# One streaming encoder layer on one core: a third natural tile, weight sums held back in issue order, other visit sizes for the adaptive product, another opening order

## The chip, the cores and the metric

The kernel runs on one core of one Trainium2 chip. Its engines work side by side, each through its own queue in order: TensorE (PE, with weight loads PEld), VectorE (DVE), ScalarE (ACT), GpSimd (POOL) and SyncE (SP), which here only issues transfers (DMAs). The metric is device time in microseconds (us), lower is better.

## The reference

One layer of an encoder is computed for two request groups: a prompt of 1024 rows and a sample of 32 rows with 512 cached rows. Width is 1024, everything is float32.

```python
ada = silu(c) @ w_ada + b_ada              # six vectors of 1024 for each group
h = rms_norm(x, g_pre_mix) * (1 + sc1) + sh1
p = h @ w_in                               # 1024 x 4256: latents, rope key, SB q, k, v, two gates
o_a = latent attention (softmax)           # 8 heads, chunk mask
o_b = stick-breaking attention             # 8 heads of 64, causal
merged = sigmoid(g_a) * (o_a @ w_proj_a) + sigmoid(g_b) * (o_b @ w_proj_b)
x = x + gt1 * rms_norm(merged @ w_out, g_post_mix)
x = x + gt2 * rms_norm(conv_ffn(rms_norm(x, g_pre_ffn) * (1 + sc2) + sh2), g_post_ffn)
```

Besides the two outputs, the new key and value rows of both branches and the last rows of the convolution are returned. The change touches the computation of `ada`, the first normalisation `h`, the part of `h @ w_in` that gives q, k and v of the stick-breaking branch, and the loads with which that branch's attention begins.

## The kernel before

Each float32 operand of the large products is split into a rounded half ("hi", ScalarE, line 96) and a remainder ("lo", VectorE, line 99), and a product is three matmuls. Most of the program is written in Tile, a language in which a planner sets the issue order of each engine from the program order and its own costs; where it says `manual_schedule`, PE, ACT and DVE keep the order of the program. Each tag of a pool has so many buffers; a tile waits until the last reader of the buffer's former tile is done, and a pool laid over the space of a released one waits tile by tile.

*Opening (`stage_h`, manual order).* Eight tiles of 128 rows of x come in. For each, `scale` takes the sum of squares on ScalarE (L136), the power on POOL (L128, L129) and the multiplication on VectorE (L414). `ada_half` is the product that gives shift and scale for one half of the columns, in eight steps whose weights are loaded as they are used (L293, L296), and then transposes (L302). `norm_T` takes four tiles of rows and half of the columns: for each of four column blocks it transposes on TensorE (`turn_x`, L315), and `put` (L324) writes scale and shift, once in full and once rounded, on ScalarE; the remainder is VectorE's. `each(n, m, ...)` runs one step of each in that order. `Plain` are the first products with plain weights (L550, read out at L73).

*The strips (`stage_in`, planned).* The product for q, k and v is made by a scheme that saves one product in eight: for each pair of 128-column strips there are seven half-size products, `step_a` to `step_g`, each of 24 matmuls (L550). Its sums of weight halves are taken on VectorE: `sum_1` (L569) adds two halves, `sums_w` (L589, L590) and `sum_4` (L594) overwrite them. `z_out` (L558, L560) reads results out of PSUM, with copies on ScalarE or sums on VectorE; steps d, e and f accumulate in one pair of banks, which is read between them. There are six such groups (n = 2 to 7, called strips 2 to 7 below). Weights of even ones lie in `wr`, of odd ones in `S`, two buffers each. `z_done` stores a finished strip. For k and v it transposes back to rows (L741), copies to a "natural" tile `nat` (L743, two buffers) and stores that (L748); for v it also splits into `hs` (L752, L753, two buffers) and stores that to `vd` (L754).

*Stick-breaking attention (`stage_sb`, PE, ACT and DVE in the written list `ORDER`).* `sb_load` (L789) loads for each of a pair's two heads the keys (KH, twice), the keys' remainder (KLz), the queries (Q, twice), and V for both. Its pool `sb` lies over those of T1, T3 and T2, the operands of steps b, e and d. In `ORDER`, f is one step of filling work from `gates`: products of the gate columns (L103 to L105). Each of the 12 gate strips has 32 of these steps and, ahead of its third block, one visit of `ada_step`: 3, 3 and 2 steps in turn, each with one load of 128 rows of `w_ada` and four matmuls (L245, loads L229, L234 for the bias). The first tile of a visit is `wa`, the others are `wr`, which the gate weights (L113) also use. The sum is added at D (L250).

## Time and profile before

| | |
|---|---|
| median of three runs | 1762.36 us (1761.33 to 1766.96) |
| the profiled execution's own time | 1761.96 us |
| its span, first to last instruction | 1759.9 us |
| granted TensorE clock over the span | 0.987 |
| PE busy / DVE busy / ACT busy / POOL busy | 1691.3 / 1260.4 / 928.5 / 300.3 us |
| stages named below (us from the start of the span) | opening and first products to about 97, strips to 251, stick-breaking attention from 251 |

A row of the waits names who waited, for whom, and us in total, times, longest. A row in order of time begins with the start and the length in us; brackets hold the idle time ahead of it on its engine and what ended it. Rows of SPq are issues of transfers. Several equal neighbours are merged (x2). A busy TensorE is not one at full clock: the granted clock stands in a column of its own.

### The profile page before, as it was taken

How to read it: one execution, taken by the hardware profiler on the slowest of the kernel's cores; microseconds unless marked ns; L12 is line 12 of the kernel's file. 1: busy time of each engine (PE TensorE's matmuls, PEld its weight loads, DVE VectorE, ACT ScalarE, POOL GpSimd, SP SyncE). 2: the span in 40 equal slices, each digit the busy share in tenths (PEclk: the TensorE clock that was granted, in tenths of full speed). 3: DMA queues.
4: the chain of work that ended last, by engine and by line, in shares of the span. 5: the costliest groups of instructions: out<-in, count | busy, mean ns of one | idle time of the engine just before them, and what ended most of it. 6: DMA issues, size and time to landing. Idle time of an engine off the chain costs nothing. (4 is left out here: it accounts for less than half of the span.)

```text
span 1759.9 us, 31441 instructions
## 1 busy us (share of the span) xinstructions
PE 1691.3 (96%) x12184; PEld 1540.8 (88%) x12184; DVE 1260.4 (72%) x2083; ACT 928.5 (53%) x1804; POOL 300.3 (17%) x622
## 2 busy tenths in 40 slices
PE   5899898999999999999999999999999999999997
PEld 2898897998999989889888879999999999977886
DVE  3585556887784477776777668977877787788556
ACT  5533334565564567767676267544444454444442
POOL 2103231211111001111100032211111111210013
PEclk8999999999999999999999999999999999999999
DMA  9335388564543222121237532343334323597753
GB/s 329 129 94 182 114 262 251 175 182 143 159 120 88 73 62 72 47 87 63 67 121 256 157 133 78 116 138 126 115 101 138 126 91 126 189 344 250 236 147 117
DMA packets 177928, 255.32 MB, mean 145 GB/s; under 512 B 14043, under 2 KB 118484, under 8 KB 176756
## 3 DMA queue, kind: packets, MB, share of 16 engines
q1 hardware_dynamic: 158900, 194.90, 35.5%
q0 software_dynamic: 18656, 58.34, 9.2%
q8 instruction: 96, 1.57, 0.4%
q14 instruction: 52, 0.43, 0.1%
q10 hardware_dynamic: 224, 0.09, 0.0%
HBM read 186.76 MB, written 65.99 MB: 144 GB/s over the span
## 5 line engine op out<-in xcount | busy, mean ns | idle before, releaser
L96 ACT ACTIVATE wh<-wr 128x1024 fp32r<-128x1024 f32 (+6 forms) x164 | 132.2, 816 | 239.0 <-PE s L2028 78.5
L99 DVE TENSOR_TENSOR wl<-wr,wh 128x1024 fp32r<-128x1024 f32 (+5 forms) x161 | 151.1, 945 | 94.7 <-ACT wh L96 93.5
L103 PE MATMUL mm<-H,wh 128*128 128x264 f32 x348 | 102.6, 295 | 0.0
L105 PE MATMUL mm<-H,wl 128*128 128x264 f32 x348 | 99.9, 287 | 0.0
L104 PE MATMUL mm<-H,wh 128*128 128x264 f32 x348 | 99.6, 286 | 0.0
L2029 PE MATMUL s<-T,wl 128*128 128x256 f32 (+1 forms) x328 | 93.7, 286 | 0.0
L2027 PE MATMUL s<-T,wh 128*128 128x256 f32 (+1 forms) x328 | 93.3, 284 | 0.0
L2028 PE MATMUL s<-T,wh 128*128 128x256 f32 (+1 forms) x328 | 93.2, 284 | 0.0
L99 DVE TENSOR_TENSOR PTl<-tr,PTh 128x512 fp32r<-128x512 f32 x100 | 68.2, 685 | 29.6 <-ACT PTh L96 29.0
L2168 DVE SCALAR_TENSOR_TENSOR u<-u,c,u 128x1058 f32<-128x1058 f32 x68 | 87.0, 1316 | 1.9 <-ACT u L2165 0.7
L99 DVE TENSOR_TENSOR wl<-S,wh 128x1024 fp32r<-128x1024 f32 (+1 forms) x58 | 60.9, 1056 | 35.5 <-ACT wh L96 35.4
L925 PE MATMUL tr<-c,A 128*128 128x128 f32 x576 | 83.8, 275 | 1.1 <-DVE A L1027 0.5
L2027 PE MATMUL tr<-T,wh 128*128 128x272 f32 (+1 forms) x272 | 77.8, 286 | 0.0
L2029 PE MATMUL tr<-T,wl 128*128 128x272 f32 (+1 forms) x272 | 77.7, 286 | 0.0
L96 ACT ACTIVATE wh<-S 128x1024 fp32r<-128x1024 f32 (+1 forms) x58 | 53.4, 926 | 45.7 <-PE s L2028 13.4
L2028 PE MATMUL tr<-T,wh 128*128 128x272 f32 (+1 forms) x272 | 77.5, 285 | 0.0
L96 ACT ACTIVATE PTh<-tr 128x512 fp32r<-128x512 f32 x100 | 59.3, 598 | 32.0 <-PE tr L925 28.6
L886 DVE TENSOR_TENSOR_SCAN M<-M,tab 128x512 f32<-128x512 f32 (+4 forms) x64 | 58.6, 916 | 21.2 <-ACT M L871 21.0
L925 PEld LDWEIGHTS tr<-c,A 128*128 128x128 f32 x576 | 65.6, 141 | 9.2 <-issue 2.1
L2029 PE MATMUL mm<-T,wl 128*128 128x256 f32 (+1 forms) x256 | 73.0, 286 | 0.3 <-DVE wl L99 0.2
L2027 PE MATMUL mm<-T,wh 128*128 128x256 f32 (+1 forms) x256 | 73.1, 286 | 0.0
L2028 PE MATMUL mm<-T,wh 128*128 128x272 f32 (+1 forms) x256 | 72.8, 285 | 0.0
(820 smaller groups left out, 6222.3 us busy)
## 6 DMA issues: line engine op xcount, KB each, us to landing
wr<-in_w_up_dram SPq DMA_DIRECT2D x44, 512.0 KB
dr<-in_w_down_dram SPq DMA_DIRECT2D x43, 512.0 KB
wr<-in_w_ada_dram SPq DMA_DIRECT2D x33, 512.0 KB
wr<-gdn SPq DMA_DIRECT2D x30, 512.0 KB
wr<-in_w_in_dram SPq DMA_DIRECT2D x27, 512.0 KB
gdn<-u POOLq DMA_DIRECT2D x23, 512.0 KB, 4.8
t<-gd SPq DMA_DIRECT2D x16, 528.0 KB
d<-in_w_down_dram SPq DMA_DIRECT2D x16, 512.0 KB
```

Source lines behind the costliest of these rows:

```text
L96: self.nc.scalar.activation(out, in_, AF.Identity, scale=scale)
L99: return self.nc.vector.tensor_tensor(out, full, hi.bitcast(F32), ALU.subtract)
L103: m(ps, lh, rh, start=start, stop=False)
L104: m(ps, lh, rl, start=False, stop=False)
L105: self.pe = m(ps, ll, rh, start=False, stop=stop).ins
L886: self.nc.vector.tensor_tensor_scan(r, r, tab[:, ::-1], 0.0, ALU.mult, ALU.max)
L925: self.nc.tensor.transpose(tr[:, (2 * s + q) * P : (2 * s + q + 1) * P], at[q][:, b * P : b * P + P], self.idt)
L2027: m(ps[:, :n], w[0][:, k], x[0][:, k, c], start=first and k == 0, stop=False, skip_group_check=True)
L2028: m(ps[:, :n], w[0][:, k], x[1][:, k, c], start=False, stop=False, skip_group_check=True)
L2029: i = m(ps[:, :n], w[1][:, k], x[0][:, k, c], start=False, stop=k == 3, skip_group_check=True)
L2168: nc.vector.scalar_tensor_tensor(y, u[:, w : w + YW], self.cvT[:, w, cc : cc + 1], y, ALU.mult, ALU.add)
```

## The change

- `nat` gets three buffers, `q1` two in place of three.
- `sum_1` is put behind the last output of the group before (`f_out`, the second L560 of `step_f`) in VectorE's issue order. For the first group there is none.
- The visits of `ada_step` for the first pair of heads do 1, 3 and 4 steps in 3, 3 and 2 turns of the fill; for the later pairs as before 3, 3 and 2. Where there are fewer steps than turns, a turn is empty; where more, the last steps fall into one turn. The fourth tile of a visit lies in an `A` buffer of the attention.
- The load for the first visit is issued after the loads of both heads in place of after V; `wa` is allocated ahead of Q and KH in the pool `sb`.
- Opening: for the first half of the columns the rounded put of every odd block goes to VectorE (`put_v`). The `scale` of tiles 4 to 7 comes between the four steps of the first `norm_T`, ahead of the first product, in place of after it. Steps of the second `norm_T` (n) and of `ada_half` (m) run n n m m n m m n m m m m in place of n m m n m m n m m n m m.

```diff
@@ ada_load
-        w = self.tl(pool, [P, D], F32, "wr") if i else self.tl(self.Sp, [P, D], F32, "wa", 1)
+        w = self.tl(*((self.Sp, [P, D], F32, "wa", 1), (pool, [P, D], F32, "wr"), (pool, [P, D], F32, "wr"),
+                      (self.At, [P, TP], F32, "A"))[i])
@@ ada_step
+        n, turns = n
...
-            if i < n - 1:
+            if i < min(n, turns) - 1:
                 yield
+        for _ in range(turns - n):
+            yield
@@ norm_T
+        def put_v(out, x, q):
+            nc.vector.tensor_scalar(out, x, g[:, q, 0:1], self.adaT[:, 0, q, 0:1], ALU.mult, ALU.add)
...
-                put(H[0][:, k, c], x, q)
+                (put if hf or k % 2 == 0 else put_v)(H[0][:, k, c], x, q)
@@ stage_h
                 n = norm(0, 0, turned)
-                each(n, n, n, n)
+                for t in range(4, 8):
+                    each(n)
+                    scale(t)
                 A.go(0, 0, "mm", 0)
-                for t in range(4, 8):
-                    scale(t)
                 n = norm(4, 0)
-                each(n, m, m, n, m, m)
-                each(n, m, m, n, m, m)
+                each(n, n, m, m, n, m, m, n, m, m, m, m)
@@ z_out
-                self.nc.scalar.copy(out[:, c], ps[:, :n])
+                r = self.nc.scalar.copy(out[:, c], ps[:, :n])
             else:
-                self.nc.vector.tensor_tensor(out[:, c], ps[:, :n], x[:, c], ALU.add)
+                r = self.nc.vector.tensor_tensor(out[:, c], ps[:, :n], x[:, c], ALU.add)
+        return r
@@ step_a
-        g["q1"] = self.z_q("q1", 3)
+        g["q1"] = self.z_q("q1", 2)
@@ sum_1
-        self.nc.vector.tensor_tensor(s, g["rb"][:, :512], g["rb"][:, 512:], ALU.add)
+        with self.tc.issue_after(self.f_out.ins) if self.f_out else ExitStack():
+            self.nc.vector.tensor_tensor(s, g["rb"][:, :512], g["rb"][:, 512:], ALU.add)
@@ step_f
-        self.z_out(g["ub"][:, :HC], g["X"], g["q1"])
+        self.f_out = self.z_out(g["ub"][:, :HC], g["X"], g["q1"])
@@ z_done
-            st = self.tl(self.Zp, [P, n * P], F32, "nat" if n > 1 else "nat1", 2 if n > 1 else 1)
+            st = self.tl(self.Zp, [P, n * P], F32, "nat" if n > 1 else "nat1", 3 if n > 1 else 1)
@@ sb_load
-                if p == 0:
-                    self.ada_w = [self.ada_load(self.W, self.At, 0, *self.ada_todo[0])]
+        if p == 0:
+            self.ada_w = [self.ada_load(self.W, self.At, 0, *self.ada_todo[0])]
@@ gates
-                        yield from self.ada_step((3, 3, 2)[i % 3], self.W, self.At, ada)
+                        yield from self.ada_step(((1, 3), (3, 3), (4, 2))[i] if i < 3 else ((3, 3), (3, 3), (2, 2))[i % 3], self.W, self.At, ada)
@@ stage_sb
-        for n, shape, dt in (("M", [P, TP + 8], F32), ("V", [P, 8, 2, P], F32R), ("Q", [P, TP], F32R), ("KH", [P, TP], F32R)):
-            self.tl(S, shape, dt, n, {"V": 1, "KH": 2, "Q": 3}.get(n))
+        for n, shape, dt in (("M", [P, TP + 8], F32), ("V", [P, 8, 2, P], F32R), ("wa", [P, D], F32), ("Q", [P, TP], F32R),
+                             ("KH", [P, TP], F32R)):
+            self.tl(S, shape, dt, n, {"V": 1, "KH": 2, "Q": 3, "wa": 1}.get(n))
```

More of the change, by code (lines that the diff above doesn't have):

```diff
@@ L335, in norm_T @@
                 put(f, x, q)
-                put(H[0][:, k, c], x, q)
+                (put if hf or k % 2 == 0 else put_v)(H[0][:, k, c], x, q)
                 self.lo(H[1][:, k, c], f, H[0][:, k, c])
                 if t0:
-                    nc.vector.tensor_scalar(edge[:, k], tr[:, 0:16], g[:, q, 0:1], self.adaT[:, 0, q, 0:1], ALU.mult, ALU.add)
+                    put_v(edge[:, k], tr[:, 0:16], q)
                     if k % 2:
@@ L400, in stage_h @@
         self.B = ((B11, B12), (B21, B22))
-        self.n_unit, self.S, self.done = 0, [], []
+        self.n_unit, self.S, self.done, self.f_out = 0, [], [], None
         self.Z = dict(B11=B11, B21=B21, B22=B22)
```

## The prediction

> **What bounds the kernel now.** I read the page's first part, then TensorE's (PE's) waits grouped by line, then the busy times of chosen stretches with their granted clock, and last the instructions in order of time around each long wait. The page first:

> ```profile
> span 1759.9 us, 31441 instructions
> ...
> PE 1691.3 (96%) x12184; PEld 1540.8 (88%) x12184; DVE 1260.4 (72%) x2083; ACT 928.5 (53%) x1804; POOL 300.3 (17%) x622
> ```

> TensorE is busy for 1691.3 of 1759.9 us, and the change takes no matmul away. All it can win is 68.6 us of idle time and what a slower clock costs after it. TensorE's waits, the longest groups that the changed lines touch:

> ```profile
> PE mm L245 <- DMA wr<-in_w_ada_dram: 6.0, 2, 5.6
> PE tr L741 <- ACT nat L743: 5.6, 3, 3.7
> PE tr L315 <- DVE x L414: 4.2, 4, 1.3
> PE mm L550 <- DVE u L560: 3.9, 1, 3.9
> ...
> PE s L816 <- DMA Q<-qld: 2.2, 1, 2.2
> ```

> They are five places: the adaptive matmuls (L245), the natural tiles (L741), the opening (L315), the strip sums (L550) and the first attention loads (L816). Each costs more than its wait, because the granted clock falls behind it. These are stretches (start:end, length, busy us per engine with counts, then granted clock, DMA share, GB/s):

> ```profile
> 22.00:37.00 15.00, 7.51 (x26) 4.11 (x28) 7.67 (x13) 11.00 (x18) 4.32 (x8) 0.64 1.05 381
> 145.40:149.40 4.00, 4.00 (x21) 4.00 (x22) 1.68 (x4) 0.58 (x1) 1.75 (x2) 0.57 0.80 282
> 198.80:204.00 5.20, 5.19 (x24) 5.19 (x25) 2.53 (x5) 0.00 (x0) 0.00 (x0) 0.53 0.00 0
> 253.70:259.00 5.30, 5.29 (x30) 5.30 (x31) 2.70 (x7) 1.56 (x6) 0.00 (x0) 0.68 1.12 400
> 273.30:279.00 5.70, 5.27 (x32) 3.58 (x32) 0.42 (x1) 0.00 (x0) 0.00 (x0) 0.52 0.72 210
> ```

> TensorE is full in the last four, at 0.57, 0.53, 0.68 and 0.52 of its clock. Lost work is the length times what is missing: 4.0 x 0.43 = 1.7, 5.2 x 0.47 = 2.4, 5.3 x 0.32 = 1.7 and 5.7 x 0.48 = 2.7 us. With the waits in front of them the places are worth: A (natural tile) 3.7 + 1.7 = 5.4; B (sum) 3.9 + 2.4 = 6.3; C (first load) 2.2 + 1.7 = 3.9; D (adaptive) 6.0 + 2.7 = 8.7 us. Two more waits of L741 make up 5.6 - 3.7 = 1.9 us.

> [...]

> **The change, part by part.** The sum is made against the profiled execution's own 1761.96 us, 0.4 us under the median of the three runs, 1762.36.

> *Third natural tile (place A).*

> ```profile
> 145.36 0.28 PE L741 MATMUL tr<-c,u 128*32 128x128 f32 x1 [3.74 <-ACT nat L743]
> ...
> 149.94 0.28 PE L550 MATMUL mm<-b12h,wh 128*128 128x256 f32 x1
> ...
> 144.72 1.26 ACT L743 COPY nat<-tr 128x512 f32<-128x512 f32 x2 [5.95 <-DMA out_dram<-nat]
> ...
> 146.63 0.43 DVE L752 CAST hs<-nat 128x512 fp32r<-128x512 f32 x1 [1.50 <-DMA vd<-hs]
> 148.15 0.42 DVE L560 TENSOR_TENSOR u<-mm,q 128x256 f32<-128x256 f32 x1 [1.09 <-DMA out_dram<-nat]
> ...
> 140.36 1.15 POOL L754 DMA_DIRECT2D vd<-hs  x2 [0.36 <-DVE hs L753]
> ```

> At 145.36 TensorE has waited 3.74 us: the third copy out of PSUM (144.72) waits until the store of the first natural tile lands. With three tiles that copy need not wait, and TensorE goes on at 141.6. What is late next is on VectorE: its cast of the third tile (146.63) waits for the store of V, issued at 140.36 from the two `hs` tiles, which nobody adds to; and the sum of step e (148.15) is queued behind that cast. Step e takes 149.94 - 145.36 = 4.6 us, less 1.7 of slow clock 2.9, so it would end at 144.5; its first output would come at 146.63 + 0.43 + 0.42 = 147.5, and step f waits 3.0 us for it. Then A wins 5.4 - 3.0 = 2.4, and 0.7 if the clock falls again for 1.7. If the planner puts the sum ahead of the cast, it wins all 5.4. Nothing in the trace decides the order; I take 3.0. The two small waits: bounds 0 and 1.9, I take 1.0, the middle. The tile's space comes from the third `q1`. The next strip's `q1` is written after step f, the last reader of the older one, so two are enough: 0.

> *Held sums (place B).*

> ```profile
> 196.99 0.69 DVE L569 TENSOR_TENSOR s<-S 128x512 f32<-128x512 f32 x1 [4.53 <-DMA S<-in_w_in_dram]
> ...
> 198.33 0.43 DVE L560 TENSOR_TENSOR u<-mm,q 128x272 f32<-128x272 f32 x1
> ...
> 201.70 0.63 PE L550 MATMUL s<-H,wh 128*128 128x256 f32 x2
> ...
> 208.45 0.29 PE L550 MATMUL s<-t1h,wh 128*128 128x256 f32 x1
> ...
> 205.59 1.16 ACT L96 ACTIVATE wh<-wr 128x512 fp32r<-128x512 f32 x2 [11.01 <-PE pv L550]
> ```

> The sum of strip 7's weight halves (L569) sits on VectorE's queue in the middle of strip 5 and waits 4.53 us for its weights; step e's second output (198.33) is queued behind it, and step f waits 3.9 us for that. Held until strip 6's step f has given its output, the sum is far behind its weights' landing. L589, which overwrites what it reads, is held with it. Cover: from the end of step f (201.70) to step b (208.45) TensorE has 6.75 us of steps g and a. In it must fit the output 0.43, the sum 0.69, ScalarE's rounding 1.16 / 2 = 0.58 and VectorE's remainder, of the sum's size, 0.69: 2.4 us. If the cover is gone, step b waits. Bounds 4.0 (2.3 us of other work of VectorE then lies in front of step e) and 6.3; I take 6.0.

> *Attention's opening (C, and the first visit of D).*

> ```profile
> SPq L789 <- PE mm L550: 21.1, 3, 20.0
> ...
> 242.29 1.15 SPq L789 DMA_DIRECT2D KH<-khd  x2
> ...
> 244.64 1.02 SPq L789 DMA_DIRECT2D Q<-qhd  x1
> ...
> 246.98 0.42 SPq L229 DMA_DIRECT2D wa<-in_w_ada_dram  x1
> ...
> 263.43 0.45 SPq L789 DMA_DIRECT2D Q<-qhd  x1
> 264.96 0.45 SPq L789 DMA_DIRECT2D Q<-qld  x1
> 266.37 0.94 SPq L229 DMA_DIRECT2D wr<-in_w_ada_dram  x2
> ...
> 263.46 0.64 PE L245 MATMUL mm<-wa,cT 128*32 128x256 f32 x8 [0.32 <-DMA wa<-in_w_ada_dram]
> ...
> 300.09 0.64 PE L245 MATMUL mm<-wr,cT 128*32 128x256 f32 x8
> ...
> 320.75 0.64 PE L245 MATMUL mm<-wa,cT 128*32 128x256 f32 x8
> ```

> SyncE's first load (KH, 242.29) waits 20.0 us for TensorE. The pool's tiles lie over T1, T3 and T2 in the order of their first allocation. By the sizes in the code, the first KH (4,096 bytes a partition) covers the end of T2, which step d of the last strip reads until that moment; its last 512 bytes are T1's. With `wa` put ahead of Q and KH, everything behind moves by 4,096 bytes: both KH and both KLz come to lie on T1, free since step b, and only Q and `wa` wait for T2. So KH (2 x 256 KB) leaves before 242.29, and Q behind it meets a shorter queue. Q left at 244.64; up to 2.35 us of that can go, plus the time of 512 KB. The wait of 2.2 us is covered by either; its clock may not be. Bounds 0 (SyncE keeps its old order) and 3.9; I take 3.0.

> Place D: the first visit now does one step, from the tile loaded ahead, and two empty turns. The two `wr` loads issued only at 266.37 are no longer needed there: 6.0 + 2.7 us. Their 16 matmuls are done at the third visit, which adds what is saved here. That visit does four steps in two turns. Its last three tiles must land by 320.75, the visit before ends at 300.09; the fourth lies in an `A` buffer. 20.7 us for 2 MB, while the loads at 263.43, 264.96 and 266.37 follow each other at 1.5 us per 256 KB, or 3 us per tile: four take 12. Covered.

> Against it stands the move of `wa` itself, from 246.98 to behind the second head's five loads (KH twice, KLz, Q twice). The matmul at 263.46 already waits 0.32 us for it. Five loads at 1.5 us are 7.3 us; the two pairs of KH that leave early give back 2.9 to 5.8; and TensorE arrives 3.9 us earlier if C goes. The first visit then waits 0.3 + 7.3 - 5.8 + 3.9 = 5.7 at best by this count, up to 8.6, in place of 0.3 + 6.0. But SyncE would no longer be stuck between loads, and with `wa` landing while the engines are less crowded the wait can vanish. Bounds: a loss of 2 and a gain of 8.7; I take 4.0, a little above the middle, since two loads of 512 KB leave this stretch.

> *Opening.*

> ```profile
> 24.41 0.77 ACT L324 ACTIVATE H<-tr,c,c 128x512 fp32r<-128x512 f32 x1
> ...
> 29.05 1.09 ACT L136 ACTIVATE jk<-x 128x1024 bf16<-128x1024 f32 x1
> ...
> 32.67 1.06 ACT L136 ACTIVATE jk<-x 128x1024 bf16<-128x1024 f32 x1
> ...
> 31.17 0.75 DVE L414 TENSOR_SCALAR x<-x,rs 128x1024 f32<-128x1024 f32 x1 [1.25 <-POOL rs L129]
> ...
> 35.57 0.75 DVE L414 TENSOR_SCALAR x<-x,rs 128x1024 f32<-128x1024 f32 x1 [0.71 <-POOL rs L129]
> ...
> 36.38 0.47 PE L315 MATMUL tr<-c,x 128*128 128x128 f32 x1 [0.99 <-DVE x L414]
> ...
> 47.48 0.38 PE L302 MATMUL s<-c,ada 128*128 128x128 f32 x2
> ```

> ScalarE is the chain: after the round of 24.41, seven puts of (29.05 - 24.41) / 7 = 0.66 us, then four squares of (32.67 - 29.05) / 3 = 1.21, then POOL and VectorE's scaling, the last at 35.57, and the transposes of the last tile at 36.38. Two puts go to VectorE: 1.3 us less before the last square, so the last scaling starts at 34.2. On VectorE each odd put (no row: 512 columns out of PSUM lie between 0.42, the 256 at 148.15, and 0.75, the 1024 out of SBUF at 31.17; I take 0.7) is queued behind a scaling that waits for POOL. Step k = 3 of the first product so moves from about 30.4 to 33.6. TensorE idles in front of it, at a clock of 0.64, but nothing needs that product yet: the four tiles are scaled at 34.9. The second group of puts (k odd, again on VectorE) and the two transposes in a row save up to another 2 us before the transposes of 47.48. Bounds: a loss of 1 (the first product ends after the scaling) and a gain of 3.5; I take 2.0, nearest to the 1.3 that the rows give.

> Sum: 3.0 + 1.0 + 6.0 + 3.0 + 4.0 + 2.0 = 19.0 us. 1761.96 - 19.0 = 1743.0 us.

> **The rivals.**

> *The adaptive tile comes late.* Place D wins nothing and loses 1: 1743 + 5 = 1748. For it: the 0.32 us at 263.46, and DMA that is full there. Against: KH leaves earlier. [...]

> *The waits move one step.* A keeps 0.7 (the V stores hold VectorE), the small waits and the opening nothing, C 1.0: 1743 + 2.3 + 1 + 2 + 2 = 1750. For it: the 1.50 us that the cast at 146.63 waits already.

> *Slower: held sums come too late.* At step b of strips 3 to 7, five times, if VectorE's queue behind step f's output exceeds the 6.75 us of cover. Each wait of x us also costs 1.7 of clock. It decides the sign when 5 (x + 1.7) passes 19 + 5.7, x = 3.2; at x = 4 it is 28.5, and 1771.5 us. Against it: 2.4 us against 6.75, and VectorE is busy 2.53 of 5.20 us in the stretch from 198.80.

> *It does not do what it says.* The strips' loop and the loads have no written order; the planner could put other work where the sums and copies were, and new waits of the old size appear: about 1760.

> **How the numbers follow.** Forecast 0.55, adaptive tile late 0.17, waits moved 0.14, no net change 0.08, sums late 0.06. All best ends together give 29.7 us less (1732), all worst 1.7 less (1760), neither likely; 1733 to 1757 leaves out the slower case and most of the unchanged one. Under 0.3% (5.3 us) a measurement here tells nothing from no change: the first three cases are faster, 0.86; the fourth the same, 0.08; the last slower, 0.06.

> **What would show it.** Right: no wait of L550 for L560 above 1 us, L569 behind the step f output; the copies L743 without 5.95 us in front of the third; the first KH load issued about 7 us before the last step d ends; one L245 group at the first visit. Wrong: a long wait of L245 for `wa`; VectorE's L752 waiting for `vd` while L550 waits for L560; L550 on `t1h` waiting for L99; clock below 0.7 in new stretches.

## The result, and the profile after

The changed kernel took 1752.52 us (median of four runs, 1746.44 to 1753.15) against 1762.11 us for the kernel before: a ratio of 0.9932 (of means, not of these medians), with an interval of 0.9904 to 0.996. A second set of five runs gave 1748.5 us and 0.992 (0.9908 to 0.9932). It is faster, by 10 to 14 us; forecast were 19.0, with a range of 1733 to 1757 us. The profiled execution took 1746.44 us. The page of the changed kernel begins:

```profile
span 1744.5 us, 31440 instructions
...
PE 1683.2 (96%) x12184; PEld 1534.4 (88%) x12184; DVE 1262.9 (72%) x2087; ACT 926.6 (53%) x1800; POOL 302.4 (17%) x622
```

Lines have moved by one to eight: L246 is the adaptive matmul (L245 before), L748 and L750 the natural tile's transposes and copy, L555 and L565 the strip product and its output, L576 the first sum, L759 the cast of V, L796 the loads of a pair, L823 the scores. TensorE's waits in the changed kernel, by line (in total, times, longest):

```profile
PE mm L246 <- DMA wa<-in_w_ada_dram: 9.1, 1, 9.1
...
PE mm L555 <- DVE H L330: 3.6, 2, 2.2
PE mm L555 <- ACT H L327: 2.1, 1, 2.1
PE mm L555 <- DVE u L565: 2.0, 2, 1.6
...
PE tr L748 <- ACT nat L750: 0.7, 1, 0.7
```

Of the five groups shown before, the two `wr` waits (6.0), four of the opening's (4.2) and the wait for Q (2.2) are gone; the natural tile's fell from 5.6 to 0.7 and the strip sums' from 3.9 to 2.0. Two are new. 3.6 us are the opening's first product, which waits for VectorE's puts; the transposes behind it lose nothing by that, for they start without a wait at 34.58 us, when the last scaling ends (33.85 + 0.75). 9.1 us, the longest, are for `wa`, the tile whose load the change moved. Stretches of the changed kernel (columns as in the prediction):

```profile
45.00:236.00 191.00, 181.99 (x1470) 177.89 (x1470) 123.45 (x203) 80.44 (x153) 47.20 (x75) 1.00 0.49 160
...
240.00:250.00 10.00, 5.62 (x44) 5.32 (x43) 6.80 (x13) 4.95 (x12) 1.63 (x7) 1.00 1.18 301
250.00:262.00 12.00, 7.33 (x41) 6.52 (x42) 4.17 (x8) 3.57 (x8) 0.56 (x1) 0.57 0.90 310
```

The strips run at full clock throughout in this execution; the wait for `wa` leaves TensorE 5.62 of 10 us busy, and the clock is 0.57 behind it. The milestones, in order of time, TensorE first, then SyncE's queue:

```profile
45.32 0.38 PE L305 MATMUL s<-c,ada 128*128 128x128 f32 x2
...
237.78 0.34 PE L823 MATMUL s<-KH,Q 128*128 128x384 f32 x1
...
254.67 1.08 PE L246 MATMUL mm<-wa,cT 128*32 128x256 f32 x8 [9.05 <-DMA wa<-in_w_ada_dram]
...
304.97 0.64 PE L246 MATMUL mm<-wa,cT 128*32 128x256 f32 x8
```
```profile
221.71 1.14 SPq L796 DMA_DIRECT2D KH<-khd  x2
...
235.09 0.56 SPq L230 DMA_DIRECT2D wa<-in_w_ada_dram  x1
236.61 10.48 SPq L235 DMA_DIRECT2D ada<-in_b_ada_dram  x4
```

The opening ends 47.48 - 45.32 = 2.2 us earlier. From there to the first score matmul the time fell from 206.23 to 192.46, by 13.8 us. From that matmul to the third adaptive visit (304.97, 320.75 before) it took 67.19 in place of 67.04 us: there nothing was won, though two of six adaptive steps are now done behind this stretch. From the third visit to the end it took 1439.6 us, 1439.1 before.

### The profile page after: what moved, and what is told of

Same layout as the page of the kernel before. It is cut to its first block, busy times and chain, and to the rows that moved or that the text cites. A ratio compares the mean times of both kernels' runs of the same rounds, so it can differ in the third digit from the quotient of the medians.

```text
span 1744.5 us, 31440 instructions
## 1 busy us (share of the span) xinstructions
PE 1683.2 (96%) x12184; PEld 1534.4 (88%) x12184; DVE 1262.9 (72%) x2087; ACT 926.6 (53%) x1800; POOL 302.4 (17%) x622
## 3 DMA queue, kind: packets, MB, share of 16 engines
q8 instruction: 96, 1.57, 0.4%
## 5 line engine op out<-in xcount | busy, mean ns | idle before, releaser
L96 ACT ACTIVATE wh<-wr 128x1024 fp32r<-128x1024 f32 (+6 forms) x164 | 132.2, 817 | 226.0 <-PE s L2036 82.1
L99 DVE TENSOR_TENSOR wl<-wr,wh 128x1024 fp32r<-128x1024 f32 (+5 forms) x161 | 151.2, 946 | 92.8 <-ACT wh L96 92.0
L99 DVE TENSOR_TENSOR PTl<-tr,PTh 128x512 fp32r<-128x512 f32 x100 | 68.1, 686 | 29.9 <-ACT PTh L96 29.3
L99 DVE TENSOR_TENSOR wl<-S,wh 128x1024 fp32r<-128x1024 f32 (+1 forms) x58 | 61.0, 1056 | 37.8 <-ACT wh L96 36.4
L96 ACT ACTIVATE wh<-S 128x1024 fp32r<-128x1024 f32 (+1 forms) x58 | 53.4, 926 | 57.0 <-PE s L2036 13.1
L96 ACT ACTIVATE PTh<-tr 128x512 fp32r<-128x512 f32 x100 | 59.3, 598 | 32.7 <-PE tr L932 29.4
L2166 POOL COPY c<-u 128x2 f32<-128x2 f32 x44 | 26.6, 605 | 260.0 <-DVE u L2112 224.9
```

What stands on the lines that cost most here:

```text
L96: self.nc.scalar.activation(out, in_, AF.Identity, scale=scale)
L99: return self.nc.vector.tensor_tensor(out, full, hi.bitcast(F32), ALU.subtract)
```

## The experiments

Three questions: what the move of `wa` costs, what each other part is worth by itself, and what is left at place A. Times are medians of four to eleven runs. Four kernels (the old visit sizes, the old allocation, the third `hs` tile, two natural tiles) ran beside a kernel before with a median of 1761.11 us, the others beside 1762.46 to 1762.72, so a difference between the two groups is uncertain by some 1.6 us.

**The changed kernel once more** (1748.5 us).

> The changed kernel once more, unaltered. Its profiled execution took 1746.44 us, its three timed ones 1752.41 to 1753.15, with a mean clock of 0.992 against 0.989 to 0.990. Theory (a spell of half clock more): 0.0025 of 1750 us is 4.4 us of lost clock; a profile of an execution of about 1752.5 us shows one spell of half clock more or a longer one than the profile at hand, somewhere behind a wait of the adaptive tile, and the same waits otherwise. Rival (a load that lands late at times): the same number of spells, and one wait for a DMA that is 4 to 6 us longer. If all executions are near 1746 or near 1752.5 the difference lay in the single execution and stays open.

The profile of an execution of 1749.45 us has the same waits (9.54 us for `wa`, 1.83 for step e's sum). But the clock fell at three places where it had not in the execution of 1746.44 us. Rows of this profile:

```profile
50.00:54.00 4.00, 4.00 (x21) 4.00 (x22) 1.86 (x2) 1.25 (x3) 0.00 (x0) 0.57 0.97 396
145.00:150.00 5.00, 5.00 (x31) 5.00 (x30) 4.10 (x9) 1.58 (x2) 2.26 (x5) 0.66 0.53 215
...
612.00:617.00 5.00, 4.94 (x26) 4.89 (x26) 2.28 (x6) 1.75 (x4) 0.00 (x0) 0.66 0.00 0
```

Each costs 4 x 0.43 = 5 x 0.34 = 1.7 us: 5.1 together, against a difference of 3.0 between the two executions. So spells account for the difference, as the theory said, and for more than its size; but they stand behind small waits and not behind the adaptive tile. Hence, below, differences of under 3 us are read from waits in the trace, not from medians.

**The load of `wa` back in its old place** (1738.42 us, ratio 0.986, 0.9845 to 0.9875).

```diff
+                if p == 0:
+                    self.ada_w = [self.ada_load(self.W, self.At, 0, *self.ada_todo[0])]
-        if p == 0:
-            self.ada_w = [self.ada_load(self.W, self.At, 0, *self.ada_todo[0])]
```

> The changed kernel with the load of the adaptive tile issued where it was before the change: behind the first head's loads and V, ahead of the second head's key, low key and query loads. Allocation, visit sizes and the opening stay changed. Theory (the tile comes late because five loads of the second head, 2.5 MB on the same queue, stand ahead of it): the wait of TensorE at the first visit falls from 9.05 us to between 0 and 4, with the clock around it above 0.76, and the kernel is 4 to 9 us faster than the changed one, near 1745. Rival 1 (the queue carries the same bytes, so the wait goes to the next load in the row): the first matmul or the transposes that need the second head's key wait instead, 3 to 8 us, and the time is within 2 us of the changed kernel. Rival 2 (the tile is late because of the B12 copies of GpSimd, not because of its place): the wait stays above 7 us and the time within 2 us.

The wait is gone. SyncE's queue, the visit, and a stretch of this kernel:

```profile
234.82 0.64 SPq L230 DMA_DIRECT2D wa<-in_w_ada_dram  x1
235.51 1.17 SPq L796 DMA_DIRECT2D KH<-khd  x2
```
```profile
248.35 0.64 PE L246 MATMUL mm<-wa,cT 128*32 128x256 f32 x8
```
```profile
240.00:260.00 20.00, 19.28 (x151) 17.83 (x151) 18.01 (x32) 12.23 (x30) 5.09 (x15) 1.00 1.17 348
```

TensorE is busy 19.28 of 20 us at full clock, and the third visit comes 297.32 - 240.58 = 56.7 us after the first scores, not 67.2. The issue time of `wa` hardly differs (234.82, 235.09); what lay ahead of it on the queue does. B12's copies by GpSimd are in both, so they are not the cause (the second rival), and the wait went to no other load (the first). The five loads that stood ahead are 256 KB each, 1.3 MB together, not the 2.5 of the expectation. The move alone costs 1748.5 - 1738.42 = 10.1 us, twice what the whole rival was priced at.

**Loads in order of need** (1739.78 us, 0.9865, 0.9852 to 0.9879). Both heads' KH and KLz, the first head's Q, `wa`, V, the second head's Q, and the bias loads last.

> The changed kernel with the first pair's loads in another order on the same queue: both heads' keys and low keys, the first head's queries, the adaptive tile, V, the second head's queries, and the four bias loads of the adaptive sum last. Theory (order of need: each load lands before its reader): no wait over 2 us at the first visit, none at the first scores, 5 to 10 us faster than the changed kernel, and not slower than the kernel that only moves the tile back. Rival (the queue is full until the second block of the gates, whatever its order): TensorE waits 3 to 8 us at the first visit all the same, or as long for the B12 tile at the gates behind it, and the time is within 2 us of the changed kernel.

```profile
245.42 0.64 PE L249 MATMUL mm<-wa,cT 128*32 128x256 f32 x8
...
250.42 0.39 PE L103 MATMUL mm<-b12h,wh 128*128 128x264 f32 x1 [0.65 <-DMA b12h<-b12h]
```

The visit has no wait, and B12 one of 0.65 us. From the first scores to the third visit it is 294.13 - 237.59 = 56.5 us, as with the load merely moved back. So two orders that put `wa` ahead of the second head's queries do equally well; bringing all the keys forward adds nothing beyond that.

**The old visit sizes** (on the kernel with the load moved back; 1746.02 us, 0.9916, 0.9902 to 0.9929).

```diff
-                        yield from self.ada_step(((1, 3), (3, 3), (4, 2))[i] if i < 3 else ((3, 3), (3, 3), (2, 2))[i % 3], self.W, self.At, ada)
+                        yield from self.ada_step(((3, 3), (3, 3), (2, 2))[i % 3], self.W, self.At, ada)
```

> The kernel that moves the adaptive tile's load back, with the old visit sizes too (three, three and two steps); allocation, opening, third natural tile and held sums stay changed. Theory (the first visit's two further tiles can only leave when the transfers of the first pair are through): TensorE waits 5 to 6 us for them again at the first visit and a spell of half clock follows, 6 to 9 us slower than with the new sizes, near 1746. Rival (with the first loads 7 us earlier, SyncE comes to these tiles earlier as well): the wait is under 2 us, the time within 2 us of 1738.42, and the visit sizes are worth nothing by themselves.

```profile
257.15 1.08 PE L246 MATMUL mm<-wr,cT 128*32 128x256 f32 x8 [6.89 <-DMA wr<-in_w_ada_dram]
```

The wait is back, 6.89 us, with half clock behind it (1.08 us for the group in place of 0.64). The visit sizes are worth 1746.02 - 1738.42 = 7.6 us by the medians, and (1762.72 - 1738.42) - (1761.11 - 1746.02) = 9.2 when each is taken against its own kernel before. So place D holds two edits of opposite sign: 7.6 to 9.2 won, 10.1 lost. This kernel has both undone, and its ratio (0.9916) cannot be told from that of the changed kernel (0.992): D as a whole is worth about nothing.

**The old allocation of `wa`** (on the same kernel; 1741.96 us, 0.9897, 0.9882 to 0.9913). `wa` leaves the list of tiles allocated ahead.

> The kernel that moves the adaptive tile's load back, with its tile allocated on first use again, behind Q and KH, so that the first KH lies over T2 as before; all else as there. Theory: the first loads leave only when the last step d is through, about 7 us later than at 224.51; TensorE waits 2 to 2.5 us for the first scores, a spell of half clock follows (1.7 us), and the adaptive tile and B12 come later too: 3 to 6 us slower than 1738.42. Rival (the early loads only fill a queue that is not needed yet): no wait over 1 us at the first scores and within 2 us.

```profile
240.89 0.41 PE L823 MATMUL s<-KH,Q 128*128 128x384 f32 x1 [1.55 <-DMA Q<-qld]
...
249.99 0.64 PE L246 MATMUL mm<-wa,cT 128*32 128x256 f32 x8 [1.18 <-DMA wa<-in_w_ada_dram]
```

The wait for the first scores returns, 1.55 us, and 1.18 us for `wa` behind it; no spell of half clock follows. That is 2.7 us by the waits and 3.5 by the medians (5.1 against each one's own kernel before). The first KH leaves at 230.08 us here, against 224.51 with the new allocation, 5.6 us earlier.

**Sums not held back** (on the changed kernel; 1758.36 us, 0.9978, 0.9967 to 0.9988).

```diff
-        with self.tc.issue_after(self.f_out.ins) if self.f_out else ExitStack():
+        with ExitStack():
```

> The changed kernel without the order that holds the first sum of weight halves behind step f's output; all else stays changed. Theory (the sum stands ahead of step f's output on VectorE and waits there for a DMA): the stalls of TensorE on VectorE's output of step f come back, four of them, 3.6 us in sum, and 2.4 us of clock with them: 4.0 to 6.3 us slower than the changed kernel. Rival 1 (the third tile has already freed VectorE's queue, and the sum's own load is in time): under 1 us. Rival 2 (waits return without their clock, since the wait of 1.57 us left in the changed kernel cost no clock): 3 to 4 us.

VectorE, and TensorE behind it, in this kernel:

```profile
191.39 0.69 DVE L576 TENSOR_TENSOR s<-S 128x512 f32<-128x512 f32 x1 [4.99 <-DMA S<-in_w_in_dram]
...
192.72 0.43 DVE L565 TENSOR_TENSOR u<-mm,q 128x272 f32<-128x272 f32 x1
```
```profile
193.22 0.60 PE L555 MATMUL mm<-b12h,wh 128*128 128x272 f32 x1 [4.35 <-DVE u L565]
```

The stall of before, sum in front of output, is back at its old place, 4.35 us, once and not four times as I had expected, and the clock falls with it:

```profile
192.00:198.00 6.00, 4.79 (x27) 4.79 (x28) 3.79 (x9) 0.00 (x0) 0.00 (x0) 0.72 0.00 0
```

Wait and clock come to 4.35 + 6 x 0.28 = 6.0 us. The third visit comes at 313.06, against 307.16 in the second profile of the changed kernel, 5.9 us later; that the two agree is partly luck, since 1.0 us of it lies in the opening (45.41 and 44.39) and the second profile has the two spells near 50 and 145 that this one has not. The medians differ by 9.9. Some of the rest is clock, far behind the strips, where the second profile of the changed kernel has one spell of 1.7 us and this one lost 10 x 0.34 = 3.4:

```profile
783.00:793.00 10.00, 10.00 (x53) 9.31 (x53) 1.48 (x5) 3.15 (x8) 0.54 (x1) 0.66 0.18 46
```

Beside it stand small waits in lines that the edit does not touch, the largest at L2373 (2.1 us in place of 1.0) and L383 (0.7). Why they come with this edit stays open, and so do 2 to 4 us of the 9.9.

**Two natural tiles and three `q1`** (on the changed kernel; 1751.69 us, 0.9948, 0.9935 to 0.9962).

```diff
-        g["q1"] = self.z_q("q1", 2)
+        g["q1"] = self.z_q("q1", 3)
-..."nat" if n > 1 else "nat1", 3 if n > 1 else 1)
+..."nat" if n > 1 else "nat1", 2 if n > 1 else 1)
```

> The changed kernel with two natural tiles and three q1 again; all else stays changed. Theory (the third copy out of PSUM waits for a store to leave the first of two tiles, and TensorE's transposes wait behind it): TensorE's waits for ScalarE's natural copies come back, three with 5 to 6 us in sum, the wait for step e's sum at the same place goes in exchange (1.6 us), and a spell of half clock of 1.7 us follows: 4 to 6 us slower than the changed kernel's 1748.5. Rival 1 (the wait moves from one engine to the other and only the clock is saved): 1 to 2.5 us. Rival 2 (the stall at this place only went to the later strips): within 1 us.

```profile
PE tr L748 <- ACT nat L750: 5.0, 3, 3.4
```

The natural tile's waits are 5.0 us again and those for step e's sum (u, L565) are gone: 5.0 against 0.7 + 2.0 is 2.3 us, the medians say 3.2, or 4.8 against each one's own kernel before. By the waits that is the upper end of the first rival, most of the wait having moved from one engine to another; the times reach into the range of the theory and do not decide.

**What is left at place A.** In the changed kernel TensorE waits 1.57 us, and VectorE, ahead of it, 2.47:

```profile
144.14 0.40 PE L555 MATMUL mm<-b12h,wh 128*128 128x272 f32 x1 [1.57 <-DVE u L565]
```
```profile
142.58 0.43 DVE L759 CAST hs<-nat 128x512 fp32r<-128x512 f32 x1 [2.47 <-DMA vd<-hs]
...
143.65 0.43 DVE L565 TENSOR_TENSOR u<-mm,q 128x272 f32<-128x272 f32 x1
```

A third `hs` tile, with one `q2` less, on the kernel with the load moved back (1739.65 us, 0.9882, 0.9867 to 0.9898):

> The kernel that moves the adaptive tile's load back, with a third hs tile (the tile of K, Q and V halves that is stored to memory), its space taken from the second q2. Theory for what is left at place A (VectorE's cast waits for the store of V to leave one of two hs tiles, with the sum of step e queued behind it): the cast's wait of 2.5 to 2.8 us and TensorE's wait for that sum (1.6 to 1.9 us, once 0.4) go, and with them the spell of half clock that some executions have there (1.7 us): 1.5 to 3.5 us faster than 1738.42. Rival (VectorE is late there by its own load, not by the wait): TensorE's wait stays over 1 us and the time is within 1 us. Second rival: the single q2 makes step d's output wait for step g of the strip before; a new wait, 1 to 3 us slower.

```profile
134.93 0.42 DVE L759 CAST hs<-nat 128x512 fp32r<-128x512 f32 x1
...
141.45 0.43 DVE L759 CAST hs<-nat 128x512 fp32r<-128x512 f32 x1 [2.98 <-DMA vd<-hs]
```
```profile
143.01 0.39 PE L555 MATMUL mm<-b12h,wh 128*128 128x272 f32 x1 [2.08 <-DVE u L565]
```

The third cast now goes through at once (134.93), and the fourth waits as long in its place. Four casts come in a burst of 9 us while a cast waits here until a store out of the ring has landed, 5.2 us from issue by the median in the changed kernel. So the mechanism was right, and the remedy wrong. The other remedy, with the outputs of the two column groups set apart (1737.02 us, 0.9858, 0.9843 to 0.9873):

```diff
-            while self.done:
+            if self.done:
                 self.z_done(*self.done.pop(0))
...
             self.step_e(g)
+            if self.done:
+                self.z_done(*self.done.pop(0))
```

> The kernel that moves the adaptive tile's load back, with the K and V outputs of a strip spread out: one column group's transposes, copies, casts and stores behind step c as before, the other's behind step e. Nothing else changes. Theory (four V tiles are cast within 9 us, and each hs tile is free only some 5 us after its store is issued, so the fourth or third cast waits whatever their number, with step e's sum behind it): TensorE's waits for the output of step e (1.95 and 0.36 us) go and with them the spell of half clock near 146: 2 to 4 us faster than 1738.42, near 1735.5. Rival (the later group now delays step f or step g by its transposes and copies): a new wait of TensorE for ScalarE's or VectorE's output of 1 to 3 us, and the time within 1.5 us or slower.

No wait of TensorE for step e's sum is left. The first scores come 235.64 - 45.31 = 190.3 us after the opening, in place of 192.5 in the changed kernel. A part is given back at the gates:

```profile
249.40 0.39 PE L103 MATMUL mm<-b12h,wh 128*128 128x264 f32 x1 [1.73 <-DMA b12h<-b12h]
```
```profile
249.00:255.00 6.00, 5.60 (x32) 5.53 (x33) 3.74 (x7) 1.61 (x4) 0.74 (x3) 0.72 1.05 373
```

TensorE is there earlier, and B12 now comes last: 1.73 us and 6 x 0.28 = 1.7 us of clock. With the loads in order of need as well (1738.88 us, 0.9858, 0.9842 to 0.9875):

> Both edits at once: K and V outputs of a strip spread out, and the first pair's loads in order of need (keys and low keys of both heads, the first head's queries, the adaptive tile, V, the second head's queries, biases last). Theory (the wait for B12 of 1.73 us and the spell of half clock behind it, which the spread kernel has at the gates, come from the second head's keys standing with B12 in the DMA engines; with the keys in front the wait was 0.65): the wait for B12 is under 1.2 us without a spell, and the time 1.5 to 3 us under the spread kernel's 1737.02, near 1734.5. Rival (all these loads need the same DMA engines, and attention now starts 2 us earlier): the wait for B12 stays over 1.5 us, or V comes late by as much, and the time is within 1 us of 1737.02.

No wait for B12 remains, and the third visit comes at 291.76, the earliest of all. Yet the time is not under the spread kernel's. In the profiled execution two spells of half clock far behind take the gain back. The first, in rows of this kernel:

```profile
755.00:765.00 10.00, 9.76 (x53) 0.80 0.11 31
765.00:775.00 10.00, 10.00 (x59) 0.69 0.17 43
```

It costs 2.0 + 3.1 us, with TensorE full and no wait above 1.0 us in front of it. What brings this spell I cannot say. These four, the load moved back, in order of need, and each with the outputs spread, cannot be told apart by time; all are 9 to 16 us under the changed kernel and some 24 under the kernel before.

**The opening.** With the old opening (1753.77 us, 0.994, 0.9923 to 0.9958), and with the new order but all puts on ScalarE (1750.71 us, 0.9932, 0.9916 to 0.9947):

> The changed kernel with the opening of the kernel before: all puts on ScalarE, the first product behind all four rounds, the scalings behind it, the transposes one at a time; all else stays changed. Theory (ScalarE's puts are the chain of the opening, the product is not): the transposes of the second adaptive half come at about 46.5 to 47.5 in place of 44.39 to 45.32, with nothing else moved: 2 to 3 us slower than the changed kernel's 1748.5. Rival (the opening's gain is taken back at the next wait, or by the spell of half clock in it): within 1 us.

> The changed kernel with all puts on ScalarE again, but the new order of the opening (each scaling behind its round, the product last, two transposes in a row). Theory (the two puts of 0.66 us that go to VectorE are what shortens the chain): most of the opening's gain goes, 1 to 2 us slower than the changed kernel's 1748.5, with the transposes of the second adaptive half at 45.7 to 46.7. Rival (the order alone does it, since the scalings and squares of the next tiles no longer stand behind the product): within 0.5 us of 44.39 to 45.32.

The transposes of the second adaptive half, first in the one and then in the other kernel:

```profile
48.47 0.38 PE L305 MATMUL s<-c,ada 128*128 128x128 f32 x2
```
```profile
44.67 0.38 PE L305 MATMUL s<-c,ada 128*128 128x128 f32 x2
```

The old order costs 3.2 to 4.1 us against 45.32 and 44.39. Part of that is clock, which differs between executions in the opening too: over 20 to 45 us it is 0.66 with the old opening here, 0.73 with the same opening in the kernel before (transposes at 47.48), and 0.80 in both profiles of the changed kernel. The kernel without held sums has the new opening at 0.73 too, and its transposes at 45.41. The kernel before, then that one:

```profile
20.00:45.00 25.00, 17.08 (x126) 8.79 (x122) 11.37 (x22) 17.13 (x26) 4.32 (x8) 0.73 0.91 319
```
```profile
20.00:45.00 25.00, 18.07 (x135) 10.89 (x135) 15.12 (x30) 14.42 (x22) 3.05 (x8) 0.73 0.87 316
45.41 0.38 PE L305 MATMUL s<-c,ada 128*128 128x128 f32 x2
```

So at a like clock the new opening is worth 47.48 - 45.41 = 2.1 us. The puts on VectorE are worth nothing there: without them the transposes come inside the range of the two profiles. By that milestone my theory for the puts falls and its rival holds. The median without them is 2.2 us above the changed kernel's, but its profiled execution lost more than that to a spell of half clock far behind (10 x 0.48 = 4.8 us from 775 on). The old opening's median is 5.3 us above that of the changed kernel, but its six runs spread from 1747.95 to 1755.67.

## Why the prediction was right, and where it was not

The sign, the range and most of the mechanism held; the size did not: at place D the first rival came (it had a chance of 0.17), not the forecast (0.55). In the order of its parts:

- **A, the third natural tile: right.** The next stall came where it was put, on VectorE's cast for the store of `vd`, with step e's sum behind it. It was 1.5 to 2.2 us and not 3.0, still above the 1 us that the prediction allowed for a sign of being right. Worth 2.3 by waits and 3.2 to 4.8 by times; predicted were 3.0 + 1.0 for the small waits, of which one of 0.7 stays.
- **B, the held sums: right.** 6.0 us by the wait and its clock, as predicted; the medians say 9.9, and the part above 6 is unexplained. The sums stand right behind step f's output and step b is not late, so the slower rival fell. (Its sign would have turned at 5 (x + 1.7) = 19, x = 2.1; the prediction does not say what the 5.7 us stand for that it adds there.)
- **C, the allocation: right.** The first KH leaves 5.6 us earlier (about 7 were named), and nothing waits at the scores. 2.7 us by the waits and 3.5 to 5.1 by times, 3.0 predicted.
- **D, the adaptive visit: wrong.** 4.0 predicted; measured are 7.6 - 10.1 = -2.5 to 9.2 - 10.1 = -0.9, at the lower bound of -2. The visit sizes came out (7.6 to 9.2, 8.7 offered). The step that failed is the choice behind the count: the count gave a wait of 5.7 to 8.6 us, and the trace has 9.05 to 9.54. I set it aside because "the wait can vanish", for which no row spoke. By the count, with the clock's 2.7 lost as before, D was between 6.3 - 5.7 = 0.6 and -2.3. The first rival named just this outcome; that its 1748 is so near the second set's 1748.5 is luck, as the first set's 1752.52 shows.
- **The opening: right in size, wrong in reason.** 2.0 predicted, 2.1 at a like clock, 2.2 and 3.1 in the two profiles. Not the two puts of 0.66 us but the new order shortens it. Whether that is the scalings and squares that no longer stand behind the product, or the two transposes in a row, no run parts. Step k = 3 of the first product did move as said, to 33.26 (said: 33.6).

With D at -2.5 to -0.9 in place of 4.0 the predicted sum is 12.5 to 14.1, and the two sets of runs show 9.6 and 14.2.

## What to carry to other kernels

When a load is put behind others on one queue, count the bytes ahead of it and believe the count; here, five loads more ahead (1.3 MB) went with a wait of 9.05 us, and issuing all of them earlier did not help the last. Two edits at one place are to be priced and tried apart, since a loss of 10.1 us here hid a gain of 7.6 or more. Where a ring of buffers waits for stores, spreading the work that fills it can do what one more buffer doesn't: here no wait of TensorE for step e's sum was left, where the added buffer left one of 2.08 us.

## What the runs showed of the hardware

```profile
PE tr L1989 <- ACT t L96: 1.8, 1, 1.8
PE mm L1213 <- DVE big L1350: 1.8, 1, 1.8
```

In this profile the clock stayed at 1.00 behind both. In the second profile of the changed kernel it fell to 0.66 behind the wait of L1213 (as at 612 us above) and stayed at 1.00 behind the other; in the kernel before it stayed at 1.00 behind the first of the two and was 0.50 from 1036.54 us on behind the second, which ended at 1035.42. Twelve waits of 3.44 to 10.07 us in the strips and behind each came with a spell: 3.74, 3.87 and 5.59 us in the kernel before, 9.05 in the changed kernel, and eight in the other runs. In the kernel before and the changed kernel three of these four spells began before the wait was over, and one 0.30 us behind it. So a wait of 1.8 us cost 5 x 0.34 = 1.7 us in one execution and nothing in another, and with several of them executions of one kernel differ by some us. The 0.68 on which the prediction priced place C was such a case too: the wait of 2.16 us had a spell behind it there, one of 2.20 us in the kernel without held sums had none.

**A load was used 19.6 us after its issue.** In the changed kernel `wa` was issued at 235.09 and used, the moment it was there, at 254.67. The four small bias loads behind it took 10.48 us just to be issued.
